# Matmul with subtraction: the tiny early store to the output moved from ScalarE's DMA queue to second place in SyncE's, with an on-chip source

## The chip, the cores and the metric

The kernel runs on one core of one Trainium2 chip. The metric is the device time of one execution in microseconds (us), the median of several runs. A separate profiled execution gives the trace; its span (208.7 us for the kernel before) runs from the first instruction to the last and is a little shorter than the device time.

## The reference

```python
def setup_inputs():
    batch, m, k, n = 16, 512, 1024, 768
    return {
        "x": np.random.randn(batch, m, k).astype(np.float32),
        "weight": np.random.randn(k, n).astype(np.float32),
        "sub_value": np.random.randn(batch, m, n).astype(np.float32),
    }

def reference(x, weight, sub_value):
    return (np.matmul(x, weight) - sub_value).astype(np.float32)
```

All batches share one weight, so this is one product of 8192 x 1024 by 1024 x 768, less a matrix of 8192 x 768. In fp32, x is 33.6 MB, the weight 3.1 MB, the subtrahend 25.2 MB and the output 25.2 MB.

## The kernel before

The 8192 rows are 64 tiles of 128 rows. Eight tiles in a row form a segment, in which one partition holds eight neighbouring rows, so that one transfer of 8 tiles moves one long run per partition.

The work on a tile of x, in order:

1. SyncE loads it into `x_ring` (16 tiles, fp32).
2. ScalarE casts it to fp16 (`cast`, line 324).
3. It is transposed: for most tiles by TensorE (`transposes`, line 342) with a copy out of PSUM by ScalarE (line 355), for every third pair of tiles by VectorE (`transposes_dve`, line 375).
4. TensorE multiplies it with the resident fp16 weights: 8 weight loads (line 404) and 16 matmuls (line 199) into PSUM.
5. VectorE subtracts (`finish`, line 424). The tile of `sub_value` was loaded into `so_ring` (32 tiles), and the result is written over it.
6. SyncE stores it to the output from `so_ring`.

The fp32 weights are staged in the last slots of `so_ring` by two transfers (line 264) and cast to fp16 by VectorE (line 269).

All large transfers, loads and stores, go through SyncE's queue, in the order of a list written by hand. They are `('x', 0, 1)`, `('w', 0, 2)`, `('x', 1, 2)`, `('w', 2, 2)` and so on: kind, first tile (or weight chunk), count. `issue()` takes from the list as long as what each transfer needs has been planned; the needed waits go with the instruction. The first eleven transfers wait for nothing. Each transfer counts up a semaphore by 16 when it has landed. The first store to the output that matters is `('o', 0, 8)`, the sixteenth entry.

Beside the list, one tiny DMA is issued at the very start on ScalarE's queue (line 177). It copies 32 floats (128 B) of every 512th row of `sub_value` into the same places of the output, 16 rows in all, and counts up the semaphore `touched`. Later stores overwrite these places; every store has a wait on `touched` among its waits:

```python
if kind == "o":
    waits.append((touched, 16))
```

At the start GpSimd clears two buffers, `idle_w` and `idle_x` (lines 178 and 179), and counts up `idle` for each. TensorE multiplies them 13 times and more while the first loads are under way (`idle`, line 434); nothing reads those products.

The program of each engine is collected in a `Queue` and written out at the end. If an instruction has several waits, all but the last become instructions of their own ahead of it (line 58).

Of the kernel before, what the change touches and what calls it, by code (L numbers as in the profile page):

```python
# [9 lines left out]
Q = 32  # L10
F32 = mybir.dt.float32
# [93 lines left out]
def kernel(  # L105
# [7 lines left out]
    nc = tc.nc  # L113

    x_flat = x.flatten_outer_dims()
    sub_flat = sub_value.flatten_outer_dims()
    out_flat = out.flatten_outer_dims()

    M_TOT, K = x_flat.shape
# [7 lines left out]
    def view(flat, at, n):  # L127

        first, size = next(one for one in SEGMENTS if one[0] <= at < sum(one))
        assert at + n <= first + size  # L130
        rows = flat[first * P : (first + size) * P].rearrange("(p j) c -> p j c", p=P, j=size)
        return rows[:, at - first : at - first + n]
# [6 lines left out]
    def sbuf(name, shape, dtype):  # L139
        return ctx.enter_context(nc.sbuf_tensor(name, shape, dtype)).ap()  # L140

    def psum(name, shape, dtype):
        return ctx.enter_context(nc.psum_tensor(name, shape, dtype)).ap()
# [16 lines left out]
    idle_x = sbuf("idle_x", [P, 512], F16)  # L160
    pt_b = psum("pt_b", [P, NPT, K], F16)
    po_b = psum("po_b", [P, NPO, 2, 512], F32)

    counter = {}
    for name in ("ident", "idle", "w", "cast", "evac", "pair", "turn", "mul", "finish"):
        counter[name] = tc.alloc_semaphore(name)
# [2 lines left out]
    def count(name):  # L169
        so_far[name] += 1  # L170
        return (counter[name], 1)

    sp, pe = Queue(nc, nc.sync), Queue(nc, nc.tensor)
    act, dve, pool = Queue(nc, nc.scalar), Queue(nc, nc.vector), Queue(nc, nc.gpsimd)

    touched = tc.alloc_semaphore("touched")
    act.add(lambda: nc.scalar.dma_start(out=out_flat[:: M_TOT // 16, :Q], in_=sub_flat[:: M_TOT // 16, :Q]), then=(touched, 16))
    pool.add(lambda: nc.gpsimd.memset(idle_w, 0.0), then=count("idle"))
    pool.add(lambda: nc.gpsimd.memset(idle_x, 0.0), then=count("idle"))  # L179
    dve.add(lambda: nc.vector.memset(ones, 1.0), then=count("ident"))  # L180
# [2 lines left out]
        out=along, data0=ones, data1=ones, initial=0.0, op0=mybir.AluOpType.mult, op1=mybir.AluOpType.add,  # L183
    ), waits=[(counter["ident"], 1)], then=count("ident"))
    dve.add(lambda: nc.vector.transpose(across, along), waits=[(counter["ident"], 3)], then=count("ident"))  # L185
    for a in range(P // Q):
        here = slice(a * Q, (a + 1) * Q)
        dve.add(lambda here=here: nc.vector.tensor_tensor(  # L188
            out=ident[here, here], in0=along[here], in1=across[here], op=mybir.AluOpType.is_equal,
# [41 lines left out]
    def lane(tag):  # L231

        for one in lanes:
            if one["tags"] <= known:
                break
        else:
            one = {"sem": tc.alloc_semaphore(f"lane{len(lanes)}"), "value": 0, "tags": set()}
            lanes.append(one)
        one["value"] += 16
        one["tags"].add(tag)  # L240
        return one["sem"], one["value"]

    def issue():
        nonlocal known, from_w
        while todo:
            kind, at, n = todo[0]
            span = set(range(at, at + n))
            old = {t - NX if kind == "x" else t - NSO for t in span}
            need, by = {
                "w": (set(), "o"),  # L250
                "x": ({t for t in old if t >= 0}, "cast"),
                "s": ({t for t in old if t >= 0}, "o"),
                "o": (span, "finish"),
            }[kind]
            if not need <= done[by]:
                return
            todo.pop(0)
            done[kind] |= span
            if kind == "w":

                first = NSO - 2 * (n_c - at)
                st = so_ring[:, first : first + 2 * n]
                sem, value = lane((kind, at))
                sp.add(lambda st=st, at=at, n=n: nc.sync.dma_start(out=st, in_=w_half[at // n]), then=(sem, 16))  # L264
                for c in range(at, at + n):
                    for r in range(2):
                        here = so_ring[:, first + 2 * (c - at) + r]
                        dve.add(
                            lambda c=c, r=r, here=here: nc.vector.tensor_copy(out=w_sb[:, c, r], in_=here),  # L269
                            waits=[(sem, value)], then=count("w"),  # L270
                        )
                        staged[first + 2 * (c - at) + r] = so_far["w"]
                    w_at[c] = so_far["w"]
                from_w |= {(("w", at), so_far["w"])}
                continue
            ring, size, flat = {
                "x": (x_ring, NX, x_flat), "s": (so_ring, NSO, sub_flat), "o": (so_ring, NSO, out_flat)
            }[kind]
            here = ring[:, at % size : at % size + n]
            there = view(flat, at, n)  # L280
            waits = []
            if kind == "x" and need:
                waits.append((counter["cast"], max(cast_at[t] for t in need)))
                last = max(need, key=lambda t: cast_at[t])
                known |= {tag for t, tag in of_x.items() if t in cast_at and cast_at[t] <= cast_at[last]}
            if kind == "s":
                for t in need:
                    waits.append(landed["o", t])
                    known.add(of_o[t])
                for t in span:  # L290
                    if t % NSO in staged:
                        waits.append((counter["w"], staged.pop(t % NSO)))
                        known |= {tag for tag, value in from_w if value <= waits[-1][1]}
            if kind == "o":
                waits.append((touched, 16))
                waits.append((counter["finish"], max(finish_at[t] for t in need)))
                known |= {of_s[t] for t in finish_at if finish_at[t] <= max(finish_at[u] for u in need)}
            sem, value = lane((kind, at))
            for t in span:
                landed[kind, t] = (sem, value)  # L300
                {"x": of_x, "s": of_s, "o": of_o}[kind][t] = (kind, at)
            if kind == "o":
                here, there = there, here
            sp.add(lambda here=here, there=there: nc.sync.dma_start(out=here, in_=there), waits, (sem, 16))  # L304

    def cast(mi):
        assert mi in done["x"]
        done["cast"].add(mi)
        x_in = x_ring[:, mi % NX].rearrange("p (g q c r) -> p g c q r", g=2, c=2, r=2)
        first = mi - mi % 2  # L310
        waits = [landed["x", mi]]
        if first in ON_DVE:
            if mi == first:
                b, before = take("x16p", N16P, mi)
                if before is not None:
                    waits.append((counter["pair"], pair_at[before]))
            to = x16p_b[:, slot["x16p", first], mi - first]
        else:
            b, before = take("x16", N16, mi)
            if before is not None:  # L320
                waits.append((counter["turn"], turn_at[before]))
            to = x16_b[:, b]
        to = to.rearrange("p (g c q r) -> p g c q r", g=2, c=2, r=2)
        act.add(lambda: nc.scalar.copy(out=to, in_=x_in), waits, count("cast"))  # L324
        cast_at[mi] = so_far["cast"]
        issue()
# [92 lines left out]
    def finish(mi):  # L419
        assert mi in done["s"]  # L420
        done["finish"].add(mi)
        o = so_ring[:, mi % NSO].rearrange("p (h n) -> p h n", h=2)
        po = po_b[:, slot["po", mi]]
        dve.add(lambda: nc.vector.tensor_tensor(  # L424
            out=o, in0=po[:, :, :NS], in1=o, op=mybir.AluOpType.subtract
        ), [landed["s", mi], (counter["mul"], mul_at[mi])], count("finish"))
        finish_at[mi] = so_far["finish"]
        issue()

    issue()  # L430


# [132 lines left out]
```

## Time and profile before

| what | value |
|---|---|
| device time, median of 3 runs | 210.57 us (210.28 to 210.61) |
| span of the profiled execution | 208.7 us |
| TensorE (PE) busy | 195.2 us, 94% |
| VectorE (DVE) busy | 127.7 us, 61% |
| ScalarE (ACT) busy | 113.1 us, 54% |
| moved by DMA | 87.08 MB, mean 417 GB/s |
| packets of SyncE's queue (q1) | 4896, 97.7% of 16 engines' span |
| packets of ScalarE's queue (q10) | 32, 0.0% |
| tiny store: issue / issue to landing | 0.61 us / 3.8 us |
| first x load: issue / issue to landing | 0.38 us / 3.6 us |

A busy share is the time in which the engine had an instruction under way, over the span. PEld is the loading of weights into TensorE. SPq and ACTq are the instruction queues of SyncE and ScalarE, where the issue of a DMA is an instruction. "Issue to landing" runs from the start of that instruction to the last of the 16 counts of the transfer's semaphore. There are 16 DMA engines; each transfer is split over them, and a packet is one run of bytes that one of them moves. Besides the tables, the trace holds each packet with queue, start, length and size, and each count of a semaphore with its time; "packet records" and "landings" in the text below mean these.

### The profile page before, as it was taken

Reading aid. Unit: us, or ns where it says so; the run is one execution under the profiler, and the core shown is the slowest. Engines: PE = TensorE matmul, PEld = TensorE weight load, DVE = VectorE, ACT = ScalarE, POOL = GpSimd, SP = SyncE. Lnnn points to the kernel's source line nnn. Section 1 sums busy time; section 2 is a strip of 40 time slices with the busy share of each in tenths; the row PEclk is TensorE's granted clock in tenths of the full one; section 3 lists DMA queues with packets and bytes.
Section 4 is the critical chain, followed back from the end, with each engine's and each line's share of the span. In section 5 each row is a group of like instructions: output and inputs, shape, how many; then the busy total and the mean of one; then the engine's idle time right before and its main releaser. Section 6 shows DMA issues by size and latency. Waiting matters only on the chain.

```text
span 208.7 us, 2605 instructions
## 1 busy us (share of the span) xinstructions
PE 195.2 (94%) x1231; PEld 75.4 (36%) x699; DVE 127.7 (61%) x224; ACT 113.1 (54%) x113; POOL 1.0 (0%) x7
## 2 busy tenths in 40 slices
PE   6789799998999999999999999999999999999950
PEld 0133344333434434433442443343344344344310
DVE  2321517945893895597399389479749938942330
ACT  3275678606674761953845676283674747616300
POOL 1000000000000000000000000000000000000000
PEclk9999999999999999999999999999999999999997
DMA  6999999999999999999999999999999999999992
GB/s 219 427 426 433 429 433 434 459 426 413 433 466 421 360 438 452 448 408 426 473 408 422 443 419 429 449 438 432 416 454 408 426 452 415 429 438 448 411 412 120
DMA packets 4932, 87.08 MB, mean 417 GB/s; under 512 B 576, under 2 KB 576, under 8 KB 960
## 3 DMA queue, kind: packets, MB, share of 16 engines
q1 hardware_dynamic: 4896, 87.03, 97.7%
q8 instruction: 1, 0.02, 0.0%
q14 instruction: 3, 0.02, 0.0%
q10 hardware_dynamic: 32, 0.00, 0.0%
HBM read 61.87 MB, written 25.17 MB: 417 GB/s over the span
## 4 chain that ended last, share of the span: by engine, by line
PE 72%; DMA 22%; ACT 2%; issue 1%; DVE 0%; SPq 0%
PE po_b L199 64%; DMA x_ring<-in_x_dram 22%; PE pt_b L342 7%; ACT x_b L324 1%; DVE so_ring L424 0%; ACT xt_b L355 0%; SPq L264 0%; SPq L304 0%; SPq L560 0%; ACT x16p_b L324 0%; SPq L137 0%
## 5 line engine op out<-in xcount | busy, mean ns | idle before, releaser
L199 PE MATMUL po_b<-w_sb,xt_b 128*128 128x384 f16 x704 | 126.0, 326 | 3.2 <-DVE w_sb L269 1.3
L424 DVE TENSOR_TENSOR so_ring<-po_b,so_ring 128x768 f32<-128x768 f32 x64 | 60.5, 956 | 60.0 <-PE po_b L199 38.6
L355 ACT COPY xt_b<-pt_b 128x1024 f16<-128x1024 f16 x44 | 44.5, 1013 | 57.2 <-PE pt_b L342 57.2
L375 DVE STREAM_TRANSPOSE xtp_b<-x16p_b 32x256 f32<-32x256 f32 x144 | 62.7, 435 | 3.5 <-ACT x16p_b L324 1.4
L199 PE MATMUL po_b<-w_sb,xtp_b 128*128 128x384 f16 x320 | 61.4, 326 | 0.5 <-DVE so_ring L424 0.2
L404 PEld LDWEIGHTS <-xt_b 128*128 128x128 f16 x352 | 34.4, 98 | 60.3 <-issue 54.8
L324 ACT CAST x_b<-x_ring 128x1024 f16<-128x1024 f32 x46 | 50.5, 1126 | 9.7 <-DMA x_ring<-in_x_dram 9.7
L342 PE MATMUL pt_b<-ident,x_b 128*128 128x128 f32 x184 | 47.6, 274 | 0.8 <-ACT x_b L324 0.7
L342 PEld LDWEIGHTS pt_b<-ident,x_b 128*128 128x128 f32 x184 | 25.3, 141 | 44.0 <-issue 35.0
L324 ACT CAST x16p_b<-x_ring 128x1024 f16<-128x1024 f32 x18 | 20.3, 1128 | 14.0 <-DMA x_ring<-in_x_dram 14.0
L404 PEld LDWEIGHTS <-xtp_b 128*128 128x128 f16 x160 | 15.7, 98 | 19.2 <-issue 17.1
L269 DVE CAST w_sb<-so_ring 128x768 f16<-128x768 f32 x8 | 3.9, 555 | 9.9 <-DMA so_ring<-in_weight_dram 9.9
L199 PE MATMUL po_b<-idle_x,idle_w 128*128 128x512 f16 x23 | 6.8, 448 | 1.7 <-POOL idle_x L179 1.7
L355 ACT COPY xtp_b<-pt_b 128x1024 f16<-128x1024 f16 x2 | 2.0, 1020 | 1.7 <-PE pt_b L342 1.7
L324 ACT ACT_TABLE_LOAD x1 | 1.3, 1283 | 1.5 <-SPq L137 1.5
L434 PEld LDWEIGHTS <-idle_w 128*128 128x128 f16 x3 | 0.3, 99 | 1.9 <-POOL idle_x L179 1.7
L188 DVE TENSOR_TENSOR ident<-along,across 32x32 f32<-32x32 f32 x4 | 0.7, 183 | 0.1
L180 DVE MEMSET ones<- 128x32 f32 x1 | 0.1, 85 | 1.0 <-SPq L137 1.0
L179 POOL MEMSET idle_x<- 128x512 f16 x1 | 0.5, 529 | 0.0
L506 ACT CAST stub<-ident 128x1 f16<-128x1 f32 x2 | 0.4, 212 | 0.0
L185 DVE STREAM_TRANSPOSE across<-along 128x32 f32<-128x32 f32 x1 | 0.2, 212 | 0.0
L483 POOL MEMSET mark<- 128x1 f32 x1 | 0.1, 99 | 24.2 <-ACT xtp_b L355 24.2
(7 smaller groups left out, 1.0 us busy)
## 6 DMA issues: line engine op xcount, KB each, us to landing
so_ring<-in_sub_value_dram SPq DMA_DIRECT2D x7, 3072.0 KB, 24.2
out_dram<-so_ring SPq DMA_DIRECT2D x7, 3072.0 KB, 26.9
x_ring<-in_x_dram SPq DMA_DIRECT2D x5, 4096.0 KB, 23.5
x_ring<-in_x_dram SPq DMA_DIRECT2D x2, 2048.0 KB, 29.1
so_ring<-in_weight_dram SPq DMA_DIRECT2D x2, 1536.0 KB, 9.5
x_ring<-in_x_dram SPq DMA_DIRECT2D x3, 1024.0 KB, 20.3
so_ring<-in_sub_value_dram SPq DMA_DIRECT2D x2, 1536.0 KB, 23.1
x_ring<-in_x_dram SPq DMA_DIRECT2D x1, 3072.0 KB, 28.0
```

The lines of the kernel that those rows point to most:

```text
L179: pool.add(lambda: nc.gpsimd.memset(idle_x, 0.0), then=count("idle"))
L188: dve.add(lambda here=here: nc.vector.tensor_tensor(out=ident[here, here], in0=along[here], in1=across[here], op=mybir.AluOpType.is_equal, ...
L199: return nc.tensor.add_instruction(mybir.InstMatmult(name=nc.get_next_instruction_name(), engine=full.engine, ins=list(full.ins), outs=lis ...
L269: lambda c=c, r=r, here=here: nc.vector.tensor_copy(out=w_sb[:, c, r], in_=here),
L324: act.add(lambda: nc.scalar.copy(out=to, in_=x_in), waits, count("cast"))
L342: pe.add(lambda: nc.tensor.transpose(words, from_, ident), waits, count("turn") if last else None)
L355: act.add(lambda: nc.scalar.copy(out=to, in_=pt_b[:, b]), waits, count("evac"))
L375: dve.add(lambda: nc.vector.transpose(xt[b * Q : (b + 1) * Q, :, a * Q : (a + 1) * Q], x16[a * Q : (a + 1) * Q, :, b * Q : (b + 1) * Q],), ...
L404: pe.add(lambda weights=weights: nc.tensor.ldweights(weights, tile_position=(0, 0)), [w for w in waits if w[0] in ready])
L424: dve.add(lambda: nc.vector.tensor_tensor(out=o, in0=po[:, :, :NS], in1=o, op=mybir.AluOpType.subtract), [landed["s", mi], (counter["mul"] ...
L434: pe.add(lambda: nc.tensor.ldweights(idle_w, tile_position=(0, 0)), [(counter["idle"], 2)])
L506: lambda t=t: nc.scalar.copy(out=stub[:, t - n_mt : t - n_mt + 1], in_=ident[:, :1]), [(counter["ident"], made)], count("cast")
```

## The change

The tiny store leaves ScalarE's queue. It becomes the second transfer on SyncE's queue, between the first tile of x and the first half of the weights. Its source is no longer `sub_value` in memory but 16 partitions of `idle_x`, which GpSimd has cleared; so it waits until both clearing instructions are done (`idle` at 2). It writes 128 floats (512 B) instead of 32 (128 B) into each of the same 16 rows. As before, later stores overwrite them and wait for `touched`. Nothing else is changed: order, waits and instructions on the other engines are the same, but for ScalarE's DMA, which is gone.

```diff
@@ -161,6 +161,7 @@
     po_b = psum("po_b", [P, NPO, 2, 512], F32)
 
+    touched = tc.alloc_semaphore("touched")
     counter = {}
@@ -173,8 +174,6 @@
-    touched = tc.alloc_semaphore("touched")
-    act.add(lambda: nc.scalar.dma_start(out=out_flat[:: M_TOT // 16, :Q], in_=sub_flat[:: M_TOT // 16, :Q]), then=(touched, 16))
     pool.add(lambda: nc.gpsimd.memset(idle_w, 0.0), then=count("idle"))
     pool.add(lambda: nc.gpsimd.memset(idle_x, 0.0), then=count("idle"))
@@ -302,6 +301,8 @@
             sp.add(lambda here=here, there=there: nc.sync.dma_start(out=here, in_=there), waits, (sem, 16))
+            if (kind, at) == ('x', 0):
+                sp.add(lambda: nc.sync.dma_start(out=out_flat[:: M_TOT // 16, : 4 * Q], in_=idle_x[:16].bitcast(F32)[:, : 4 * Q]), [(counter["idle"], 2)], (touched, 16))
```

The store exists to write into the output once, early, before the first large store needs it. In the new place it comes from the queue, and from the side of the chip, that the large stores use.

## The prediction

> **What bounds the kernel now.** I read the page first, for its busy shares and its 40 slices.
>
> ```profile
> span 208.7 us, 2605 instructions
> PE 195.2 (94%) x1231; PEld 75.4 (36%) x699; DVE 127.7 (61%) x224; ACT 113.1 (54%) x113; POOL 1.0 (0%) x7
> ...
> DMA  6999999999999999999999999999999999999992
> GB/s 219 427 426 433 429 433 434 459 426 413 433 466 421 360 438 452 448 408 426 473 408 422 443 419 429 449 438 432 416 454 408 426 452 415 429 438 448 411 412 120
> ```
>
> PE and the DMA engines are both full nearly from end to end. The slices are 5.2 us long; between the first and the last, only one is weak: 360 GB/s in the fourteenth (67.8 to 73.0 us). Second, the chain that ended last:
>
> ```profile
> PE 72%; DMA 22%; ACT 2%; issue 1%; DVE 0%; SPq 0%
> ```
>
> The chain is DMA first (loads of x up to 48.6 us) and PE from there to 201.4 us. It does not say what holds up the last landing, so third, the tail in stretches of 1 us (columns: stretch and length; busy us of PE, PEld, DVE, ACT, POOL with instruction counts; PE clock, DMA share, GB/s):
>
> ```profile
> 202.40:203.40 1.00, 0.00 (x0) 0.00 (x0) 0.00 (x0) 0.00 (x0) 0.00 (x0) 1.00 1.06 445
> 203.40:204.40 1.00, 0.00 (x0) 0.00 (x0) 0.00 (x0) 0.00 (x0) 0.00 (x0) 1.00 0.95 387
> 204.40:205.40 1.00, 0.00 (x0) 0.00 (x0) 0.00 (x0) 0.00 (x0) 0.00 (x0) 1.00 0.43 175
> 205.40:206.40 1.00, 0.00 (x0) 0.00 (x0) 0.00 (x0) 0.00 (x0) 0.00 (x0) 0.67 0.17 71
> 206.40:207.40 1.00, 0.00 (x0) 0.00 (x0) 0.00 (x0) 0.00 (x0) 0.00 (x0) 0.50 0.04 15
> ```
>
> All computing is over at 202.34 (last subtraction, 201.38 + 0.96). Then 16 engines, later fewer and fewer, drain what is queued. The landing times of the last store, by engine, run from 204.81 to 207.41: one of the 16 is 2.6 us behind the first. That laggard, not PE, sets the end: it has a backlog from the start on, and its time is its bytes plus every stall it met. The spread of one transfer's 16 landings was under 0.5 us up to 32.6 us, 1.85 us at 38.9 (just after an instruction fetch of 16 KB at 34.6), 1.78 us at 63.1 and 2.55 us at 74.0.
>
> So fourth, the weak slice:
>
> ```profile
> 65.00:67.00 2.00, 2.00 (x16) 0.91 (x8) 0.96 (x1) 1.31 (x2) 0.00 (x0) 1.00 0.80 344
> 67.00:68.00 1.00, 1.00 (x9) 0.44 (x4) 0.00 (x0) 1.00 (x2) 0.00 (x0) 1.00 1.21 524
> 68.00:69.00 1.00, 1.00 (x9) 0.37 (x4) 0.43 (x1) 1.00 (x2) 0.00 (x0) 1.00 1.20 492
> 69.00:70.00 1.00, 1.00 (x9) 0.54 (x5) 0.99 (x3) 1.00 (x2) 0.00 (x0) 1.00 1.52 492
> 70.00:71.00 1.00, 1.00 (x9) 0.42 (x4) 0.97 (x3) 0.78 (x1) 0.00 (x0) 1.00 0.20 66
> 71.00:72.00 1.00, 1.00 (x8) 0.35 (x4) 0.97 (x3) 0.23 (x1) 0.00 (x0) 1.00 0.81 344
> ```
>
> Packets count where they start: from 70 to 71 us almost none starts. The packet records say why: the last 32 KB packets of x tiles 24 to 31 take 1.34 to 1.76 us where the others take 1.213, and the laggard's takes 2.51. Summed over the normal length that is 8.0 us, or 0.5 us for each of 16 engines, and 1.3 us for the laggard. The next packets in the queue are those of the first big store, out tiles 0 to 7. No later store is preceded by such a stall. Nothing else in the run looks like it except the first loads: the packets of x tile 0 take 0.18 to 0.97 us where 0.159 is normal (together 8 us over, again 0.5 us an engine).
>
> Last, the head, where the edit is (start, length, instruction):
>
> ```profile
> 0.90 0.61 ACTq L177 DMA_DIRECT2D out_dram<-in_sub_value_dram  x1
> 0.94 0.38 SPq L304 DMA_DIRECT2D x_ring<-in_x_dram  x1
> 1.08 0.53 POOL L179 MEMSET idle_x<- 128x512 f16 x1
> 1.37 0.43 SPq L264 DMA_DIRECT2D so_ring<-in_weight_dram  x1
> ...
> 4.55 1.11 ACT L324 CAST x_b<-x_ring 128x1024 f16<-128x1024 f32 x1 [1.73 <-DMA x_ring<-in_x_dram]
> ...
> 8.30 1.97 DVE L269 CAST w_sb<-so_ring 128x768 f16<-128x768 f32 x4 [5.83 <-DMA so_ring<-in_weight_dram]
> ```
>
> **What the Trainium skill says.** DMA: Bandwidth & Descriptors, section Queues, rings and completion order: each DMA engine has a ring per issuing queue, takes descriptors of one ring in order, and goes round between the rings it has work in. The trace agrees: the 16 packets of 128 B from ScalarE's queue (3.77 to 4.20 us) stand, engine by engine, between the last packet of x tile 0 and the first of the weights. The same page, Specifications: first byte about 0.6 us after issue on this path, and writes under 512 B are done as read-modify-write. Here the first packet of x starts at 1.98, 1.04 us after its issue began; I use 1.04. The new store has rows of 512 B, the old one of 128 B. The same page, Anatomy of one DMA: most of the fixed cost is the receipt of the write, HBM the slowest. The trace shows a small difference: 0.32 us from the completion packet to the count for x in SBUF, about 0.5 us for the tiny store. No page speaks of a cost of a queue's first store.
>
> **The change part by part.**
>
> *ScalarE's DMA is removed.* Its issue took 0.61 us (0.90 to 1.51). The table load behind it moves up by that, but the first cast waits for x until 4.55: no gain. On the DMA engines 0.013 + 0.009 us each go away.
>
> *A store is put second in SyncE's queue.* It reads 16 rows of the zeroed idle_x, so it waits for both memsets. They end at 1.61; PE, which waits for the same count, starts at 1.66. Queued behind it are the first weights and nine more loads, and behind these VectorE's weight casts and PE. Its issue costs between 0.33 (the shortest on this queue) and 0.61 us (ScalarE's like it). The weights' issue then starts at 1.66 + 0.33 to 0.61 + 0.05 = 2.04 to 2.32 instead of 1.37, 0.7 to 0.95 us later. With 1.04 us to the first packet they can run from 3.1 to 3.4. The engines finish x tile 0 between 3.77 and 4.20. So the delay lies beside the transfer of x, with 0.4 to 0.7 us to spare: 0. All later early issues have more room (the second x load, issued at 1.85, is needed after 7.4).
>
> *Its packets* are one of 512 B per engine, between 0.013 us (128 B) and 0.121 us (3 KB), plus 0.009: about 0.03 us, against 0.022 removed. Nothing. Behind big stores, following loads start within 6 ns of the completion packet, so the wait for HBM's receipt does not block a ring.
>
> *The first store of the loads' queue* now comes at about 4 us, not at 70. If the 0.5 us stall belongs to that (first store from this queue, or from SBUF), it moves to the head. There it meets the start-up of x, when engines are slow anyway: its descriptor is there from about 2.7 us, and the slow packets last until about 3.2. I cost it there at 0.0 to 0.5 us, and take 0.5. At 70 us the laggard keeps 1.3 us. Net for the engine that sets the end: 1.3 - 0.5 = 0.8; ends 0.0 and 1.3. The second-latest engine landed at 206.70; if it lost 0.5 us at 70 like most and pays 0.5 in the head, it stays at 206.7, and the gain is trimmed to the 0.7 between 207.41 and 206.70. PE does not forbid it: the first engines land the last store at 204.81.
>
> **The rivals.**
> A, forecast: the stall at 70 us is the queue's first store, and comes cheaper in the head. 210.57 - 0.7 = 209.9. For it: it stands right before the first store and only there, and hits all 16 engines. Against: the tiny store of before had already written into the output, so a first touch of that memory is no explanation; it must be the queue or the direction.
> B, no change: the stall has another cause and stays, or moves to the head at full price on every engine; loads stay hidden. 210.5. For it: every edit I can price is hidden or under 0.03 us.
> C, slower: the stall stays and the head gets worse. Either x finishes sooner without ScalarE's packets and the weights come late, or the store holds up the ring behind it, up to the whole 0.95 us of delayed issue. 210.57 + 0.3 to 0.9, say 211.1. For it: DMA has no idle time in which to make up a late start. Against: the 0.4 us to spare.
>
> **How the numbers follow.** A 0.44, B 0.30, C 0.26. B is within 0.2% (0.42 us) by its nature, A and C beyond, so faster 0.44, same 0.30, slower 0.26. The low end, 209.2, is A with all 1.3 us kept; the high end, 211.1, is the middle of C and leaves out its late tail.
>
> **What would show it.** Right: no weak slice near 70 us, x packets there all near 1.21 us, a spread of landings below 2 us after it, and an earlier last landing. The weights' issue starts near 2.2 and their cast still near 8.3. Wrong: the same dip of GB/s before the first big store (B), or weights cast at 8.8 or later and a gap in the DMA share from 3 to 5 us (C).

## The result, and the profile after

| | before | changed |
|---|---|---|
| device time, median | 210.45 us (210.28 to 210.61, 4 runs) | 211.59 us (211.03 to 211.83, 4 runs) |
| ratio to before | | 1.005, 95% interval 1.0028 to 1.0072 |
| span of the profiled execution | 208.7 us | 209.7 us |
| first weights: last landing | 8.28 us | 10.36 us |
| last matmul ends | 201.34 us | 202.35 us |
| last store: first and last of the 16 landings | 204.81 and 207.41 us | 205.51 and 208.46 us |

The change makes the kernel half a per cent slower, where the forecast was a gain of 0.7 us (209.9). First the page of the changed kernel: busy shares, slices and the chain.

```profile
span 209.7 us, 2605 instructions
PE 195.6 (93%) x1231; PEld 76.0 (36%) x699; DVE 128.0 (61%) x224; ACT 113.3 (54%) x113; POOL 1.0 (0%) x7
...
DMA  6999999999999999999999999999999999999992
GB/s 198 363 437 429 431 424 429 431 427 445 441 433 456 417 408 441 455 419 439 442 419 431 422 445 431 445 419 420 452 417 442 436 431 422 431 441 436 414 388 102
...
PE 84%; DMA 9%; SPq 1%; DVE 1%; issue 0%; POOL 0%; POOLq 0%; DVEq 0%
```

The weak slice has moved: the fourteenth, at 70 us, is no longer weak (417 instead of 360), but the second (5.2 to 10.5 us) is: 363 instead of 427. The busy DMA row hides it, because an engine that waits on a stretched packet counts as busy. The chain now has steps of GpSimd's clearing at its start, which the store waits for; before it had none.

The head of the changed kernel in order of time (start, length, instruction):

```profile
0.94 0.38 SPq L303 DMA_DIRECT2D x_ring<-in_x_dram  x1
1.64 0.35 SPq L305 DMA_DIRECT2D out_dram<-idle_x  x1
2.04 0.41 SPq L263 DMA_DIRECT2D so_ring<-in_weight_dram  x1
...
4.50 1.11 ACT L325 CAST x_b<-x_ring 128x1024 f16<-128x1024 f32 x1 [2.32 <-DMA x_ring<-in_x_dram]
...
10.38 1.97 DVE L268 CAST w_sb<-so_ring 128x768 f16<-128x768 f32 x4 [7.92 <-DMA so_ring<-in_weight_dram]
11.46 2.72 PE L198 MATMUL po_b<-w_sb,xt_b 128*128 128x384 f16 x8 [3.24 <-DVE w_sb L268]
```

The store waits for the clearing until 1.64, as forecast; the weights are issued at 2.04 instead of 1.37. But their cast starts at 10.38 instead of 8.30: 0.67 us of delay at the issue became 2.08 at the landing. The same stretch by microseconds, first of the kernel before, then of the changed one (columns as in the prediction: the last two are DMA share and GB/s, the one ahead of them the PE clock):

```profile
4.00:5.00 1.00, 1.00 (x5) 0.00 (x0) 0.00 (x0) 0.45 (x1) 0.00 (x0) 1.00 1.01 415
5.00:6.00 1.00, 1.00 (x6) 0.14 (x1) 0.00 (x0) 0.66 (x1) 0.00 (x0) 1.00 1.05 442
6.00:7.00 1.00, 1.00 (x8) 0.43 (x4) 0.00 (x0) 0.36 (x1) 0.00 (x0) 1.00 1.01 430
7.00:8.00 1.00, 1.00 (x6) 0.10 (x1) 0.00 (x0) 0.65 (x1) 0.00 (x0) 1.00 0.89 377
```

```profile
4.00:5.00 1.00, 1.00 (x4) 0.00 (x0) 0.00 (x0) 0.50 (x1) 0.00 (x0) 1.00 0.73 299
5.00:6.00 1.00, 1.00 (x6) 0.10 (x1) 0.00 (x0) 0.61 (x1) 0.00 (x0) 1.00 1.19 393
6.00:7.00 1.00, 1.00 (x9) 0.47 (x5) 0.00 (x0) 0.25 (x1) 0.00 (x0) 1.00 1.18 369
7.00:8.00 1.00, 1.00 (x6) 0.10 (x1) 0.00 (x0) 0.76 (x1) 0.00 (x0) 1.00 0.67 258
...
11.00:12.00 1.00, 0.54 (x2) 0.15 (x1) 1.00 (x3) 0.00 (x0) 0.00 (x0) 0.69 1.09 463
12.00:13.00 1.00, 1.00 (x4) 0.15 (x1) 0.35 (x1) 0.06 (x1) 0.00 (x0) 0.50 1.03 438
```

From 4 to 5 us the DMA share is 0.73: engines stand idle. The packet records, chained so that each packet starts where the one before it on its engine ended, give four engines that are done with x tile 0 by about 3.8 us and have no packet until 5.1; their first packets of weights then take 1.5 us instead of 0.46. From 6.6 to 7.9 twelve of the 16 engines have packets of 0.8 to 1.0 us. Summed over the 16 engines from 3.9 to 9 us, 4.7 us are idle (before: 0.0), and the packets of weights and what follows take 11.5 us over their normal length (before: 0.8). PE idles for 3.24 us ahead of the weights, and its clock is halved from 11.4 to 14.8 us.

The stretch at 70 us, whose dip carried the forecast:

```profile
69.00:70.00 1.00, 1.00 (x9) 0.36 (x4) 0.42 (x1) 1.00 (x2) 0.00 (x0) 1.00 0.99 426
70.00:71.00 1.00, 1.00 (x8) 0.55 (x5) 0.99 (x3) 1.00 (x2) 0.00 (x0) 1.00 1.14 492
71.00:72.00 1.00, 1.00 (x9) 0.41 (x4) 0.97 (x3) 0.76 (x1) 0.00 (x0) 1.00 0.80 344
```

The dip is gone: 492 where it was 66 GB/s. And the tail:

```profile
202.40:203.40 1.00, 0.00 (x0) 0.00 (x0) 0.94 (x1) 0.00 (x0) 0.00 (x0) 1.00 0.99 418
203.40:204.40 1.00, 0.00 (x0) 0.00 (x0) 0.00 (x0) 0.00 (x0) 0.00 (x0) 1.00 0.73 304
204.40:205.40 1.00, 0.00 (x0) 0.00 (x0) 0.00 (x0) 0.00 (x0) 0.00 (x0) 1.00 0.86 353
205.40:206.40 1.00, 0.00 (x0) 0.00 (x0) 0.00 (x0) 0.00 (x0) 0.00 (x0) 0.78 0.35 144
206.40:207.40 1.00, 0.00 (x0) 0.00 (x0) 0.00 (x0) 0.00 (x0) 0.00 (x0) 0.50 0.13 52
207.40:208.60 1.20, 0.00 (x0) 0.00 (x0) 0.00 (x0) 0.00 (x0) 0.00 (x0) 0.50 0.03 10
```

As before, a few engines drain last, only a microsecond later: from 205.4 on the share falls to 0.35, 0.13 and 0.03.

### The profile page after: what moved, and what is told of

Its sections match the earlier page's. It is cut to its first block, busy times and chain, and to the rows that moved or that the text cites. A ratio compares the mean times of both kernels' runs of the same rounds, so it can differ in the third digit from the quotient of the medians.

```text
span 209.7 us, 2605 instructions
## 1 busy us (share of the span) xinstructions
PE 195.6 (93%) x1231; PEld 76.0 (36%) x699; DVE 128.0 (61%) x224; ACT 113.3 (54%) x113; POOL 1.0 (0%) x7
## 4 chain that ended last, share of the span: by engine, by line
PE 84%; DMA 9%; SPq 1%; DVE 1%; issue 0%; POOL 0%; POOLq 0%; DVEq 0%
PE po_b L198 76%; DMA so_ring<-in_sub_value_dram 9%; PE pt_b L343 9%; DVE so_ring L425 1%; SPq L303 0%; SPq L263 0%; POOL idle_x L178 0%; SPq L305 0%; POOL idle_w L177 0%; POOLq L561 0%; DVEq L58 0%; SPq L137 0%
## 5 line engine op out<-in xcount | busy, mean ns | idle before, releaser
L405 PEld LDWEIGHTS <-xt_b 128*128 128x128 f16 x352 | 34.6, 98 | 62.3 <-issue 57.3
L198 PE MATMUL po_b<-idle_x,idle_w 128*128 128x512 f16 x23 | 7.3, 473 | 1.7 <-POOL idle_x L178 1.7
```

The source lines that it names most:

```text
L198: return nc.tensor.add_instruction(mybir.InstMatmult(name=nc.get_next_instruction_name(), engine=full.engine, ins=list(full.ins), outs=lis ...
L405: pe.add(lambda weights=weights: nc.tensor.ldweights(weights, tile_position=(0, 0)), [w for w in waits if w[0] in ready])
```

## The experiments

Two theories stood at the start. T1: the store in the loads' rings makes the loss (its packets, its direction, or the receipt of its writes). T2: the late issue of the weights makes it; engines finish x tile 0, find no packet of weights, and run dry. T3 came later: PE's halved clock. All ratios are to the kernel before, measured beside each run. The times are medians, and a ratio is not the quotient of two medians.

| run | time, us | ratio, 95% interval | idle 3.9 to 9 us | weights landed |
|---|---|---|---|---|
| e1 no store | 210.54 | 1.0000 (0.9992 to 1.0008) | | 8.26 |
| e2 queue alone | 211.87 | 1.0048 (1.0031 to 1.0066) | 11.3 us | 11.08 |
| e3 source alone | 210.60 | 0.9999 (0.9991 to 1.0007) | | 8.44 |
| e4 delay alone, 2.06 | 211.66 | 1.0040 (1.0027 to 1.0053) | 2.2 us | 10.81 |
| e5 store third | 210.53 | 1.0001 (0.9993 to 1.0009) | | 8.35 |
| e6 store twelfth | 210.58 | 1.0002 (0.9994 to 1.0010) | | 8.38 |
| e7 delay, 1.64 | 210.74 | 1.0002 (0.9992 to 1.0011) | 0.0 us | 8.54 |
| e8 delay, 2.50 | 211.39 | 1.0041 (1.0027 to 1.0054) | 5.7 us | 10.08 |
| e9 two tiles first | 210.56 | 0.9997 (0.9989 to 1.0005) | | 9.51 |
| e10 two tiles first, changed | 210.43 | 0.9989 (0.9981 to 0.9998) | 0.3 us | 9.56 |
| e11 changed, PE kept busy | 211.83 | 1.0042 (1.0025 to 1.0058) | 3.3 us | 10.89 |
| e12 changed, one execution | 210.39 | | 2.4 us | 10.69 |
| e13 changed, 6 runs | 211.81 | 1.0085 (1.0059 to 1.0110) | 8.8 us | 10.59 |
| e14 as e10 | 210.40 | 0.9993 (0.9982 to 1.0003) | 5.5 us | 10.50 |
| e15 as e9, no store | 210.47 | 1.0003 (0.9995 to 1.0012) | | 9.32 |

Idle is engine time summed over 16 engines in the one profile of each run, where it was worked out.

**Taking the change apart (e1 to e4).** e1 takes the store out of the kernel before, with the waits for it.

```diff
-    act.add(lambda: nc.scalar.dma_start(out=out_flat[:: M_TOT // 16, :Q], in_=sub_flat[:: M_TOT // 16, :Q]), then=(touched, 16))
...
-                waits.append((touched, 16))
```

> The tiny store and the waits for it are taken out of the kernel before. If the dip at 70 us is the first store of SyncE's queue, it stays (0.3 to 0.6 us an engine, right before the first big store), and the head is as before: weights cast at 8.3 us, time 210.3 to 210.7. If the tiny store on ScalarE's queue takes part of that cost away today, the dip here is larger than 8 us in sum over the engines and the time above 210.7. If the tiny store's own traffic is what disturbs the head, the head here is better than before: weights cast before 8.1.

The old store does nothing to the time, and the dip at 70 us stays. e2 has the changed place with the old source and no wait:

```diff
+                sp.add(lambda: nc.sync.dma_start(out=out_flat[:: M_TOT // 16, :Q], in_=sub_flat[:: M_TOT // 16, :Q]), then=(touched, 16))
```

> The store is second in SyncE's queue, but still copies 128 B a row from sub_value in memory and waits for nothing. If the queue makes the cost (first store out of this queue's rings), the first weights land at about 10.4 us as in the changed kernel, the dip at 70 us is gone, and the time is 211.2 to 211.8. If the source on the chip makes it, or the later issue of the weights (here only some 0.4 us later, not 0.67), the head is as before (landing at 8.3), the dip at 70 us stays, and the time is 210.3 to 210.7.

The whole loss is there without the new source. But the store's issue took 0.61 us here, so the weights were issued at 2.04 all the same, and T1 and T2 stay together. The dip at 70 us was still there in this profile, which the first theory did not expect. e3 has the changed source in the old place:

```diff
+    act.add(lambda: nc.scalar.dma_start(out=out_flat[:: M_TOT // 16, : 4 * Q], in_=idle_x[:16].bitcast(F32)[:, : 4 * Q]), [(counter["idle"], 2)], (touched, 16))
```

> The store stays on ScalarE's queue but has the changed kernel's source and size: 512 B a row from the cleared buffer, after the wait for it. SyncE's order is as before. If the direction (on-chip buffer to memory) makes the cost, packets of the first weights stretch after 4 us as in the changed kernel, the dip at 70 us is gone, time 211.0 to 211.8. If the queue or the delay makes it: head and dip as before, 210.3 to 210.7.

The source costs nothing. e4 puts no store into SyncE's queue; it is the kernel before, with a wait that holds the weights back to 2.06 us.

```diff
-                sp.add(lambda st=st, at=at, n=n: nc.sync.dma_start(out=st, in_=w_half[at // n]), then=(sem, 16))
+                sp.add(lambda st=st, at=at, n=n: nc.sync.dma_start(out=st, in_=w_half[at // n]), [(counter["ident"], 6)], (sem, 16))
```

> The kernel before, in which the issue of the first weights waits for a count on VectorE that comes at 2.05 us, so that it is issued about 0.7 us later, as in the changed kernel; no store in SyncE's queue. If the delay makes the loss, the weights land 0.5 us or more later than 8.28 and the time is 211.0 to 211.6. If the 0.4 us to spare of the prediction hold, weights land at 8.3 to 8.4, the time is 210.3 to 210.7, and the dip at 70 us stays.

The issue of the first weights, and VectorE's cast of them:

```profile
2.06 0.33 SPq L264 DMA_DIRECT2D so_ring<-in_weight_dram  x1
...
10.83 1.97 DVE L269 CAST w_sb<-so_ring 128x768 f16<-128x768 f32 x4 [8.36 <-DMA so_ring<-in_weight_dram]
```

The delay alone costs 0.40%, against 0.50% for the whole change. Its 22 executions fall into two groups: nine from 210.54 to 211.06 and thirteen from 211.57 to 212.55. The profiled one (210.80) is of the low group: a single engine ran dry, for 2.4 us.

**The place, and the size of the delay (e5 to e8).** e5 moves the changed store behind the first weights, e6 behind the eleventh transfer.

```diff
+                if at == 0:
+                    sp.add(lambda: nc.sync.dma_start(out=out_flat[:: M_TOT // 16, : 4 * Q], in_=idle_x[:16].bitcast(F32)[:, : 4 * Q]), [(counter["idle"], 2)], (touched, 16))
```

> The changed kernel's store, same source and wait, put behind the first weights instead of ahead of them; the weights are issued at 1.37 us as before, and only the second x load and what follows are late. If the loss is the late issue of the weights (DMA engines run dry after x tile 0), all is as in the kernel before: weights cast at 8.3, time 210.2 to 210.7. If the store's packets or its write receipt in the loads' rings make the loss, the time stays at 211.2 to 211.8, with idle or stretched packets after the store.

```diff
-            if (kind, at) == ('x', 0):
+            if (kind, at) == ('s', 8):
```

> The same store as the last of the early transfers in SyncE's queue, so that its packets run at about 44 us. If late issue is the cause of the loss: 210.2 to 210.7 and an undisturbed head. For the dip before the first big store: if it is the cost of the first store of on-chip data in this queue, the dip at 70 us is gone and one near 44 us takes its place; if it is not, the dip stays at 70.

Both are as fast as before. In e5 the weights are issued first and the store behind them:

```profile
1.38 0.42 SPq L263 DMA_DIRECT2D so_ring<-in_weight_dram  x1
1.85 0.42 SPq L265 DMA_DIRECT2D out_dram<-idle_x  x1
...
8.37 1.97 DVE L270 CAST w_sb<-so_ring 128x768 f16<-128x768 f32 x4 [5.90 <-DMA so_ring<-in_weight_dram]
```

One place further back, the same store in the same rings is free, so T1 falls, and T2 stands: e4 has the loss without the store, e5 the store without the loss. The dip at 70 us is there in both, though the queue's first on-chip store now comes earlier. For e6:

```profile
69.00:70.00 1.00, 1.00 (x9) 0.50 (x5) 0.99 (x3) 1.00 (x2) 0.00 (x0) 1.00 0.85 262
70.00:71.00 1.00, 1.00 (x9) 0.43 (x4) 0.97 (x3) 0.73 (x1) 0.00 (x0) 1.00 0.86 295
```

e7 and e8 are e4 with other counts, 4 and 8, so that the weights are issued earlier and later.

```diff
-[(counter["ident"], 6)]
+[(counter["ident"], 4)]
```

> The kernel before with the first weights issued some 0.27 us later (wait for a count that comes at 1.62 us). If an engine loses only when its ring runs dry after x tile 0, this has room: no engine pauses between x tile 0 and the weights, time 210.2 to 210.7. If every 0.1 us of later issue costs in proportion (0.84 us of time for 0.67), it is 0.3 us slower than before, about 210.9.

```diff
-[(counter["ident"], 6)]
+[(counter["ident"], 8)]
```

> The kernel before with the first weights issued at about 2.5 us, 1.1 us later. If engines that run dry restart one by one 1 to 2.5 us later, now all 16 run dry, the weights land at 10.5 or later for all of them, and the time is 211.8 to 213. If the loss is in proportion to the delay, it is 211.8 to 212. If the delay is only a plain shift beside 0.4 us to spare: 211.3.

The issues, of e7 and then of e8:

```profile
0.94 0.38 SPq L304 DMA_DIRECT2D x_ring<-in_x_dram  x1
1.64 0.33 SPq L264 DMA_DIRECT2D so_ring<-in_weight_dram  x1
```

```profile
0.94 0.38 SPq L304 DMA_DIRECT2D x_ring<-in_x_dram  x1
2.50 0.33 SPq L264 DMA_DIRECT2D so_ring<-in_weight_dram  x1
```

Issue at 1.64 costs nothing, and no engine pauses. Issue at 2.06 costs 0.40%, at 2.50 0.41%: in these three points a threshold, not a slope. The time of e8 by itself (211.39) would also fit the plain shift beside 0.4 us to spare, for which 211.3 was expected. But then e4, issued 0.69 us late, would lose 0.29 us or 0.14%, and it lost 0.27 to 0.53%. The figures for engines that run dry, 211.8 to 213 us and weights at 10.5 or later, failed for e8. In its profile most engines paused, by at most about 1 us, and had first packets of up to 1.86 us, but they stayed together (landings spread over 1.37 us, against 2.96 in e4). Nine engines had nothing left to do from 3.94 us at the latest. The first packets of weights on the 16 engines start between 4.09 and 4.82 us: 1.59 us after the issue began at the earliest, 2.32 at the latest.

**Room, clock and repetition (e9 to e15).** e9 and e10 put two tiles of x into the first transfer, with the old and the changed store.

```diff
-    ('x', 0, 1), ('w', 0, 2), ('x', 1, 2),
+    ('x', 0, 2), ('w', 0, 2), ('x', 2, 1),
```

> The kernel before with two tiles of x in the first transfer instead of one (and one instead of two in the third). It is the base for the next run: x tile 0 arrives about 1.2 us later, the weights too; 210.6 to 211.9.

> The changed kernel with the same two tiles in the first transfer. The weights are issued just as late as in the changed kernel, but the engines are busy with x until about 5 us. If the loss comes from engines that run dry after the first transfer, this is within 0.1% of the run with two tiles and the old store. If the store itself or the late issues behind it cost, it is slower than that by 0.3 to 0.5%.

With 0.5 MB more ahead of the weights the late issue costs nothing. In e10's profile the engines hardly paused; in e14's, below, they did (5.5 us), and the time was no worse.

> The changed kernel with 12 more idle multiplications (2.6 us) while PE waits for the weights, so that the PE clock is not lowered. If PE's lost time at half clock makes the loss, the time falls to about 210.6 to 211.0. If the engine that drains last makes it, the time stays at 211.3 to 211.8 although the last matmul ends earlier.

e11 changes one number of the changed kernel:

```diff
-    idle(7)
+    idle(19)
```

The PE clock stayed at full speed through the head in its profile, and the time did not fall: T3 is not the cause. Two profiles below agree: e12, the shortest execution, has the halved clock from 11.6 to 15.0 us, and e13, a long one, does not have it. My picture of an earlier last matmul was wrong as well: it ended at 202.85, 0.50 us later than in the first profile of the changed kernel, and the first weights had landed 0.53 later.

> The changed kernel once more, for a second profile. If dry engines are its rule, some of the 16 pause for over 0.5 us between x tile 0 and the weights here too, and the weights land after 9.5 us; 211.0 to 211.9. For the dip at 70 us: gone again if the change removes it, there if the first profile was chance.

> The changed kernel, timed many times. If the loss depends on which engines run dry, the times fall into two groups, one near 210.4 to 211.0 and one near 211.5 to 212.3, with a median in between or in the upper group. If it is a plain shift, they lie within 0.4 us of 211.6 and the 210.39 of the single execution stays an outlier.

Eleven executions of the changed kernel in all: 210.39 once, 211.03 to 211.83 four times, 211.62 to 213.56 six times. The last six hold one of 213.56, which raises their ratio. Eleven are too few to show two groups; with e11, whose thirteen fall into 210.57 to 211.07 (five) and 211.68 to 212.33 (eight), and e4, there are two.

> Two tiles in the first transfer and the changed kernel's store, repeated. If the gain of 0.1% is real: ratio to the kernel before 0.998 to 0.9995 again, and the dip at 70 us weak again. If it was chance: 0.9995 to 1.001.

> Two tiles in the first transfer and no tiny store at all. If the store brings the 0.1%, this is at 210.5 to 210.7 and has the dip at 70 us. If the wider first transfer brings it, this is at 210.3 to 210.5 as well.

The gain of 0.1% with two tiles and the changed store is not settled: 0.9989 once, 0.9993 with 1 inside the interval the second time. Without the store there is none. The dip was absent in e14 and present in e15. No version beat the kernel before clearly.

**What makes an execution long.** e12's execution was short though its weights landed at 10.69 and PE ended later than in the long first profile. The last subtraction of the changed kernel's first profile, and then that of e12:

```profile
202.38 0.96 DVE L425 TENSOR_TENSOR so_ring<-po_b,so_ring 128x768 f32<-128x768 f32 x1 [1.64 <-PE po_b L198]
```

```profile
202.62 0.96 DVE L425 TENSOR_TENSOR so_ring<-po_b,so_ring 128x768 f32<-128x768 f32 x1 [1.64 <-PE po_b L198]
```

PE was 0.24 us later and the last landing 1.13 us earlier (207.33 against 208.46). So PE does not set the end. The ledger is in the landings: how much later than in the kernel before the last of a transfer's 16 engines was, in us, along the list of transfers.

| transfer (last landing before) | changed | e13 | e11 | e2 | e8 | e12 | e4 |
|---|---|---|---|---|---|---|---|
| first weights (8.28) | 2.08 | 2.31 | 2.62 | 2.80 | 1.81 | 2.42 | 2.53 |
| s tiles 8 to 15 (46.17) | 0.82 | 1.24 | 1.26 | 1.88 | 1.11 | 1.05 | 1.18 |
| x tiles 24 to 31 (74.02) | -0.34 | 0.08 | 0.08 | 1.64 | 1.17 | -0.12 | 0.39 |
| s tiles 48 to 55 (154.01) | 0.14 | 0.14 | 0.45 | 1.58 | 1.16 | -0.17 | 0.32 |
| out tiles 56 to 60 (204.60) | 1.05 | 1.14 | 1.44 | 1.62 | 1.47 | -0.10 | 0.36 |
| last store (207.41) | 1.05 | 1.15 | 1.45 | 1.59 | 1.46 | -0.07 | 0.34 |
| time of that execution | 211.52 | 211.62 | 211.91 | 212.06 | 211.95 | 210.39 | 210.80 |

In five of the seven, the 2 to 2.6 us of the head are all but repaid by 74 us: the laggard of the kernel before has by then lost as much elsewhere, after an instruction fetch at 34.6 us and in the dip at 70. In e12 and e4 it ends there. e2 and e8 have the dip themselves (9.7 and 12.1 us in sum over the engines, before 8.0), so 1.64 and 1.17 us are still missing at 74 us and 1.59 and 1.46 at the end.

In the three other long profiles the difference comes back, by 0.9 to 1.0 us from 154 to 204.6 us. It grows with the stores: by 0.21 to 0.29 us with each of those of out tiles 32 to 39, 40 to 47 and 48 to 55, and not with the load of s tiles 56 to 63 between them (-0.05). The packet records have something of that size in every kernel: in the stores, one engine takes about 940 ns for many 24 KB packets where 912 is normal. Each of the 17 profiles has 45 to 51 packets of 24 KB that take 920 to 970 ns, nearly all in stores, 26 to 31 of them after 165 us; they follow each other back to back, as on one engine. 8 x 28 ns = 0.22 us in a store of 8 tiles.

Is that engine the last? The landings say so. In the first profile of the changed kernel, in e13 and in e11, the slow engine's last packet in each of the four stores of out tiles 24 to 55 is followed by its completion packet, and 0.50 to 0.53 us later comes the last of the store's 16 landings. In the kernel before, in e12 and e4 that engine's landing is the 12th to 15th of the 16, so its slowness is hidden; in e2 and e8 it is the 11th to 15th, and another engine ends last. Compared with the kernel before, the slow engine ends the store of out tiles 48 to 55 later by 1.9 to 2.3 us in the three profiles, by 1.6 in e2 and e8, by 0.7 in e12 and not at all in e4. That it was one of those that ran dry fits this in size; the records do not name engines, so this last step is worked out and not shown.

## Why the prediction was wrong

**The bound** was right: the engine that drains last sets the end, not PE. e12 against the first profile shows it.

**The store's wait and issue** were right: 1.64 against 1.66 us, an issue of 0.35, the weights at 2.04 (forecast 2.04 to 2.32).

**"With 1.04 us to the first packet they can run from 3.1 to 3.4"** failed, and with it the 0.4 to 0.7 us to spare and the cost of 0. The 1.04 us were those of the earliest packet of the first transfer, issued alone into an idle queue. For the second, e8 showed 1.59 us at the earliest and 2.32 at the latest. From 2.04 that gives 3.63 to 4.36, and in the changed kernel the engines are free from 3.66 on: room for some of them and not for others. For e7 (1.64) it gives 3.23 to 3.96, with the engines free from 3.80, and none paused. I also took a missed start to cost only its own length. It cost more: twelve engines had their first weights by 4.17 us, but four only at 5.09 to 5.15, some 3 us after the issue, and these packets took 1.5 us instead of 0.46. So 0.67 us of late issue became 2.08 at the landing. Why an engine that has run dry waits so much longer than the others stays open.

**The first store of the queue** failed as an explanation. The dip at 70 us went away, as forecast, and a stretch of long packets on most engines from 6.6 to 7.9 us came. But e5 and e6 have such a store early in the same rings and keep the dip. The dip was absent or weak (at most 1.6 us in sum over the engines, where the others but e4 have 6 to 12) in all six profiles with the changed store in second place, and weak (2.3 us) in e4, which has no store there. What makes it stays open, so that it went as forecast was luck. Its worth to the laggard was right in size: the difference of the last landing to before went from +0.88 at 63.1 us to -0.34 at 74.0, a gain of 1.2 us against the 1.3 of the forecast. It was spent on the head. So in the changed kernel the dip and the loss are two things: e2 has the loss and keeps the dip.

**Rival C** was the right one by half of its mechanism, weights that come late, and I held against it just the spare time that was not there. Its signs came: a cast at 10.38 and a DMA share of 0.73 from 4 to 5 us. That the stall at 70 us stays, it had wrong. The receipt of the write was rightly cleared: e5 shows no loss.

**Edits priced at nothing** were nothing: removal of ScalarE's DMA (e1), source and size (e3).

## What to carry to other kernels

When a queue feeds a pipeline that never rests, the second issue matters as much as the first: whatever is put between two early transfers must leave the next one's packets in the rings before the first is done, and that lead time is to be measured on the queue as it is then, not on the first transfer. A harmless DMA, with its wait, belongs behind the transfers that the start depends on. And where the end is set by one of 16 DMA engines, add up each engine's losses: the same stall costs nothing on one engine and its full length on another.

## What had not been expected of the hardware

- From the start of an issue to the first packet on any engine: 1.04 us for the first transfer of the run. For the second, in e8, where engines stood idle: 1.59 us to the first engine's, 2.32 to the last one's.
- An engine that found its ring empty paused for 0.3 to 2.4 us, and its next packet of 12 KB often took 1.0 to 1.9 us instead of 0.46.
- In each of the 17 profiles 45 to 51 packets of 24 KB, nearly all in stores and by their times on one engine, took about 940 instead of 912 ns.
- An instruction fetch of 16 KB at 34.6 us took 0.93 us on one engine, and that engine's next packet 1.11 instead of 0.61. The spread of a transfer's landings went from 0.42 to 1.85 us, and the engine did not catch up.
